# Recurrence gates as per-head products on quarters of the PE array, with the gated unit and the pool branch a step later and squares on ACT

## The chip, the cores and the metric

The kernel runs on one core of a Trainium2 chip. The metric is the device time of one execution in microseconds, the median of several runs. The time before is 2156.85 us, the median of 3 runs that lie between 2155.75 and 2157.89.

## What is computed

One block of a hybrid network on 2048 tokens of width 1024, in fp32: a modulated norm, a token mix of three branches, an output projection, then a convolutional feed-forward part. The change lies in the branches of the token mix: a two-way linear recurrence whose gates are 64 x 64 products per head, a pooling branch with one product per group, and a gated unit that mixes tokens inside chunks of 128.

```python
def block_diag(xh, w, b):
    y = jnp.einsum('blhi,hij->blhj', xh, w)
    return y.reshape(y.shape[0], y.shape[1], -1) + b

def rglru_coeffs(xf, w_a, b_a, w_x, b_x, lam):
    xh = xf.reshape(B, L, N_HEADS_A, HEAD_A)          # 8 heads of 64
    r = jax.nn.sigmoid(block_diag(xh, w_a, b_a))
    i = jax.nn.sigmoid(block_diag(xh, w_x, b_x))
    log_a = -LRU_C * r * jax.nn.softplus(-lam)
    a = jnp.exp(log_a)
    bterm = jnp.sqrt(-jnp.expm1(2.0 * log_a)) * (i * xf)
    return a, bterm                                    # h[t] = a[t] h[t-1] + bterm[t], both ways

def gmlp_group(z, norm_g, w_s, b_s):
    z = jax.nn.gelu(z)
    u, v = z[..., :D_C], z[..., D_C:]
    vn = (v - mean(v)) * rsqrt(var(v) + EPS) * norm_g
    s = jnp.einsum('gij,bnjgc->bnigc', w_s, vn_in_chunks_of_128) + b_s
    return u * s

def token_mix(z, y_rec, ...):
    ya = jax.nn.gelu(z[..., D_A:2 * D_A]) * y_rec
    yb = pool_group(...)        # mean over 2, 4, 8 or 16 tokens minus z, one product per group
    yc = gmlp_group(...)
    return jnp.concatenate([ya, yb, yc], axis=-1) @ w_out
```

## The kernel before, in words

Features lie on partitions, tokens on the free axis; tokens go in four chunks of CH = 512. Large products run as fp32 split into two f16 halves: `mm3` (L357 to L361) makes three f16 matmuls per 128 inputs, 24 for one output tile of a chunk. Small products (gates, pool, the token mix of the gated unit) run in fp32 directly.

The program is written with a scheduler that sets each engine's order from its own model of time; what comes ahead in the program has priority. `ORDER` (L38) is the list of steps that a loop walks through: `x` normalises a chunk, `c` is the recurrence of the 256 context tokens, `a` the projection and convolution of the recurrence's input, `f` and `b` a recurrence unit forward or backward for a chunk and a pair of head tiles (P is tiles 0 and 1, Q is 2 and 3), `G` the gelu gates with their squares, `g` a step of the gated unit, `p` a step of the pool branch, `m` steps of the later modulation, `i` and `w` weight preparation.

A recurrence unit (`lru_units`) calls `coeffs` for two head tiles: rp (L443) and ip (L444) are fp32 products of a 128 x 128 block-diagonal weight (two heads of 64 on the diagonal) with 512 tokens, ACT makes two sigmoids, then exponentials and roots with a table load between the kinds, POOL and DVE combine (L461, L463), and DVE scans (L479). There are 16 such units of two tiles, 8 forward and 8 backward, and the context has 8 sets of half width.

`gmlp` makes, for each of 8 steps, two tiles of 128 tokens: projection uv, gelu, normalisation on DVE, then the token mix sp (L623), bias and product on DVE, four transposes tp (L632) and a copy yc (L635) with its squares on ACT. `pool_br` (L539) projects a chunk (pl), adds shifted copies on DVE (L562 to L580) and multiplies the result, pb, with its weight (pp, L535); the product's result yb is read by DVE and squared there. `gates` (L639) multiplies the gelu of a projection gt with Y and squares the product. `vsumsq` (L153) squares and sums on DVE, `sumsq` (L150) on ACT. `wout_stats` squares the eight tiles of w_out, `prep_out` splits them in two f16 halves with `split` (DVE, L312 and L313); `split_ag` (L317 to L319) does the same with two ACT Copies and one POOL subtraction.

Of the kernel before, what the change touches and what calls it, by code (L numbers as in the profile page):

```python
# [18 lines left out]
CH = 512  # L19
# [21 lines left out]
m6 b3Q G3P p m6 w4 b2P G3Q p m6 w4 b2Q G2P p m6 w2 b1P G2Q p m6 w2 b1Q G1P p  # L41
# [27 lines left out]
def block_kernel(ctx: ExitStack, tc: tile.TileContext, x, xT, ctx_d, ctxT, cc, crow, cols_d, wm01, bm01, wmT,  # L69
# [104 lines left out]
    gwt = mix.tile([128, 4, 4, 128], F32, name="gwt")  # L174
# [47 lines left out]
    def stats_first(xt):  # L222
        acc = early.tile([128, CH], F32, tag="acc", name="acc")
# [216 lines left out]
    def coeffs(j, d, xa, w, c=None, bank=None):  # L440
        bank = pB if bank is None else bank
        rp, ip = bank("rp"), bank("ip")
        T.matmul(rp[:, :w], gwt[:, j, 2 * d, :], xa, start=True, stop=True)  # L443
        T.matmul(ip[:, :w], gwt[:, j, 2 * d + 1, :], xa, start=True, stop=True)  # L444
# [3 lines left out]
        act(i[:, :w], ip[:, :w], AF.Sigmoid, bias=col("bx", 4 * d + j))  # L448
# [90 lines left out]
    def pool_br():  # L539
        W = CH + 16  # L540
        for pt in range(2):
            prev = None
            yb = []
            for n in range(NCH + 1):
# [53 lines left out]
    def gmlp():  # L598
        ws = wslot["uv"]
        for tp in range(8):  # L600
            n, r = divmod(tp, 2)
            guvt = mix.tile([128, 2, CH], F32, tag="guv", bufs=2, name="guv")
            guv = [guvt[:, i, :] for i in range(2)]
            for i in range(2):
                t0 = tp * 256 + i * 128
                ps = pA("uv")
                mm3(ps, lambda k: hT[:, 0, k, t0:t0 + 128], lambda k: hT[:, 1, k, t0:t0 + 128],
                    lambda k: ws[k // 2][:, 0, k % 2, :], lambda k: ws[k // 2][:, 1, k % 2, :])
                act(guv[i], ps, AF.Gelu_apprx_tanh, scale=inv[:, 10:11])
                bst = small.tile([128, 6], F32, tag="bst", name="bst")  # L610
                V.bn_stats(bst, guv[i][:, 256:512])
                mv = small.tile([128, 2], F32, tag="mv", name="mv")
                V.bn_aggr(mv, bst)
                rs = small.tile([128, 1], F32, tag="rsv", name="rsv")
                rsqrt(rs, mv[:, 1:2], 1, 1.0)
                v = guv[i][:, 256:512]
                V.tensor_scalar(v, v, mv[:, 0:1], rs, op0=OP.subtract, op1=OP.mult)
                V.tensor_tensor(v, v, gnr, op=OP.mult)
                if i == 0:
                    yield  # L620
            sp = pC("sp")
            for g in range(4):
                T.matmul(sp[:, g * 128:(g + 1) * 128], wst[:, g, :], guvt[:, :, 256 + g * 64:320 + g * 64], start=True, stop=True)  # L623
            sv = sp.rearrange("p (g i c) -> p g i c", g=4, i=2)
            tp_ps = pC("tp")
# [608 lines left out]
```

## Time and profile before

| what | value |
|---|---|
| median of 3 runs | 2156.85 us (2155.75 to 2157.89) |
| profiled execution | 2155.6 us |
| span of the profile | 2153.8 us |
| PE busy | 2022.0 us, 94% of the span |
| DVE busy | 1593.2 us, 74% |
| ACT busy | 1194.6 us, 55% |
| POOL busy | 610.1 us, 28% |
| mean granted clock of PE | 0.972 of full speed |

Busy shares are means over stages with different limits. The page's 40 slices show PE at 6 to 9 tenths over the first quarter of the span and at 9 or more from there to the last slices; DVE stands at 9 tenths only in slices 7, 8 and 10. The first quarter holds the context, the forward and the backward recurrences; the output projection runs from about 553 to 770 us, the feed-forward part after it.

### The profile page before, as it was taken

To read this page: it belongs to the slowest core of one execution; us is meant where nothing else is said; L and a number is where in the kernel's file an instruction comes from. 1 tells how busy PE (TensorE), PEld (TensorE's weight loads), DVE (VectorE), ACT (ScalarE), POOL (GpSimd) and SP (SyncE) were. 2 spreads that over 40 slices of the span, in tenths; PEclk is the share of its full clock that TensorE was granted. 3 is DMA by queue.
4 is the path that set the end of the run, shared out by engine and by line. 5 is a ranking of instruction groups with operands and counts; after the bars stand their busy time and mean duration, and the time that the engine had idled before them with its cause. 6 is when DMAs were issued, how large, how long until landed. Compare 5 with 4: busy or idle time off the path is not lost.

```text
span 2153.8 us, 24277 instructions
## 1 busy us (share of the span) xinstructions
PE 2022.0 (94%) x9215; PEld 933.4 (43%) x9215; DVE 1593.2 (74%) x2214; ACT 1194.6 (55%) x1665; POOL 610.1 (28%) x457
## 2 busy tenths in 40 slices
PE   6878989788899998999999999999999999999995
PEld 1433444333455443444444444444444444444442
DVE  5687788999655359978667776867777686777876
ACT  4676756455254555656565554655556465555453
POOL 1233334445155510101121121212112121221156
PEclk8889999998999999999999999999999999999998
DMA  7521152512433210315455454544545454454248
GB/s 297 183 88 74 69 166 89 180 35 85 135 136 114 79 64 20 130 66 132 89 117 98 79 124 72 108 78 102 94 88 100 74 103 88 100 95 69 40 157 156
DMA packets 73480, 224.78 MB, mean 104 GB/s; under 512 B 7442, under 2 KB 18066, under 8 KB 68498
## 3 DMA queue, kind: packets, MB, share of 16 engines
q0 software_dynamic: 21312, 77.60, 21.4%
q1 hardware_dynamic: 52052, 145.64, 19.6%
q8 instruction: 72, 1.18, 0.2%
q14 instruction: 44, 0.36, 0.1%
HBM read 120.45 MB, written 102.76 MB: 104 GB/s over the span
## 4 chain that ended last, share of the span: by engine, by line
PE 55%; DVE 3%; POOL 1%; DMA 1%; ACT 1%; issue 1%; POOLq 0%; SPq 0%; DVEq 0%; ACTq 0%
PE up L359 12%; PE up L360 12%; PE up L361 12%; PE dn L1054 6%; PE dn L1056 6%; PE dn L1055 6%; DVE cv L1011 2%; DMA hT<-accd 1%; POOL hT L1069 0%; DVE hT L1086 0%; DVE hT L1060 0%; DMA wm<-in_wmT_dram 0%; POOL fms L159 0%; PE sct L121 0%; POOL out_dram L1087 0%
## 5 line engine op out<-in xcount | busy, mean ns | idle before, releaser
L1011 DVE SCALAR_TENSOR_TENSOR cv<-z,cols,cv 128x1008 f32<-128x1008 f32 (+3 forms) x704 | 870.4, 1250 | 276.6 <-ACT cv L1005 188.7
L359 PE MATMUL up<-hT,uw 128*128 128x512 f16 x1408 | 534.1, 379 | 2.6 <-ACT z L846 2.6
L361 PE MATMUL up<-hT,uw 128*128 128x512 f16 x1408 | 534.1, 379 | 0.0
L360 PE MATMUL up<-hT,uw 128*128 128x512 f16 x1408 | 534.1, 379 | 0.0
L1071 POOL DMA_DIRECT2D accd<-dd x132 | 114.2, 865 | 704.1 <-ACT dd L1065 697.9
L846 ACT ACTIVATE z<-up,upinv 128x512 f32<-128x512 f32 x176 | 120.5, 685 | 311.2 <-PE up L361 310.8
L1065 ACT ACTIVATE dd<-dn,gdi 128x512 f32<-128x512 f32 x320 | 214.2, 680 | 115.0 <-PE dn L1056 107.5
L1054 PE MATMUL dn<-dw,gs 128*128 128x512 f16 x704 | 267.2, 380 | 7.1 <-ACT dd L1065 5.3
L1055 PE MATMUL dn<-dw,gs 128*128 128x512 f16 x704 | 267.5, 380 | 0.0
L1056 PE MATMUL dn<-dw,gs 128*128 128x512 f16 x704 | 265.8, 380 | 0.0
L360 PEld LDWEIGHTS <-uw 128*128 128x128 f16 x1408 | 137.8, 98 | 167.5 <-issue 3.6
L359 PEld LDWEIGHTS <-uw 128*128 128x128 f16 x1408 | 139.0, 99 | 164.7 <-issue 0.6
L361 PEld LDWEIGHTS <-uw 128*128 128x128 f16 x1408 | 137.8, 98 | 166.5 <-issue 0.6
L832 POOL TENSOR_TENSOR uw<-ur,uw 128x2048 f16<-128x2048 f32 x22 | 89.5, 4070 | 168.9 <-ACT ur L831 168.9
L135 ACT ACT_TABLE_LOAD x77 | 98.8, 1283 | 47.4 <-PE rp L443 28.8
L1005 ACT ACTIVATE cv<-z,cols 128x1024 f32<-128x1024 f32 x88 | 106.0, 1206 | 2.0
L1055 PEld LDWEIGHTS <-gs 128*128 128x128 f16 x704 | 68.8, 98 | 86.8 <-issue 9.5
L1054 PEld LDWEIGHTS <-gs 128*128 128x128 f16 x704 | 72.2, 103 | 78.8 <-issue 0.8
L1056 PEld LDWEIGHTS <-gs 128*128 128x128 f16 x704 | 68.9, 98 | 83.5 <-issue 0.6
L986 POOL TENSOR_TENSOR dw<-dr,dw 128x1024 f16<-128x1024 f32 x22 | 46.4, 2127 | 141.8 <-PE dn L1056 100.3
L150 ACT ACTIVATE junk<-g 128x1024 bf16<-128x1024 f32 x44 | 46.3, 1053 | 59.9 <-DVE g L1019 59.9
L878 PE MATMUL wo<-wo,ysp 128*128 128x512 f16 x256 | 77.1, 383 | 1.0 <-ACT gm L807 1.0
(302 smaller groups left out, 3076.7 us busy)
## 6 DMA issues: line engine op xcount, KB each, us to landing
accd<-dd POOLq DMA_DIRECT2D x132, 512.0 KB, 5.1
ur<-in_wup_dram SPq DMA_DIRECT2D x22, 1024.0 KB, 5.6
wm<-in_wmT_dram SPq DMA_DIRECT2D x64, 256.0 KB, 2.9
dr<-in_wdn_dram SPq DMA_DIRECT2D x22, 512.0 KB, 4.6
hT<-in_wm_dram SPq DMA_DIRECT2D x8, 1024.0 KB, 14.4
xt<-in_xT_dram SPq DMA_DIRECT2D x8, 1024.0 KB, 7.1
ro<-in_wout_dram SPq DMA_DIRECT2D x16, 512.0 KB, 3.8
xr<-in_x_dram SPq DMA_DIRECT2D x16, 512.0 KB, 3.6
```

The source lines that it names most:

```text
L135: ins = A.activation(out_, in_, func, **kw).ins
L359: T.matmul(ps, wh(k), hh(k), start=(k == 0), stop=False)
L360: T.matmul(ps, wh(k), hl(k), start=False, stop=False)
L361: T.matmul(ps, wl(k), hh(k), start=False, stop=(k == KT - 1))
L846: A.activation(z[:, ab, b * 8:(b + 1) * 8, :], ps.rearrange("p (r x) -> p r x", x=64), AF.Identity, scale=upinv[:, c:c + 1])
L1005: A.activation(t, z[:, ab, r0:r0 + 16, :].rearrange("p r x -> p (r x)"), AF.Identity, bias=col("fcb", c + NP * ab), scale=wt(0, 0))
L1011: V.scalar_tensor_tensor(o, z[:, ab, ya + dy:yb + dy, xa + dx:xb + dx], wt(dy, dx), o, op0=OP.mult, op1=OP.add)
L1054: T.matmul(ps[h], hi, wh, start=i == 0, stop=False)
L1055: T.matmul(ps[h], hi, wl, start=False, stop=False)
L1056: T.matmul(ps[h], lo, wh, start=False, stop=i == n - 1)
L1065: A.activation(d[:, h * CH:(h + 1) * CH], ps[h], AF.Copy, scale=di)
L1071: G.dma_start(accd[t], d, accum_op=OP.add)
```

## The change

The gate weights keep only the 64 x 64 blocks, loaded by eight DMAs. For each set, rp and ip are four products, each on one quarter of the array; the two halves of ip lie swapped in its bank, and two sigmoids of 64 partitions swap them back. A step of the gated unit ends during the next one: sp follows the next tile's first projection, tp the second; its results go back into guv, which has three buffers in place of two. A pool step's product and squares are issued after the next step's projection. The squares of gates, pool and w_out move from DVE to ACT, and the split of w_out to ACT and POOL. gg has two buffers in place of three, acc uses the ring of xs, and the tile yc is dropped.

```diff
@@ ORDER
-m6 b3Q G3P p ... m6 w2 b1P G2Q p m6 w2 b1Q G1P p
+m6 b3Q G3P p ... m6 w2 b1P G2Q p m6 w2 b1Q G1P p g g
@@
-    gwt = mix.tile([128, 4, 4, 128], F32, name="gwt")
+    gwt = mix.tile([128, 4, 4, 64], F32, name="gwt")
+    HALVES = (slice(0, 64), slice(64, 128))
@@ stats_first
-        acc = early.tile([128, CH], F32, tag="acc", name="acc")
+        acc = early.tile([128, 2, CH], F32, tag="xs", bufs=2, name="acc")[:, 0, :]
@@ coeffs
-        T.matmul(rp[:, :w], gwt[:, j, 2 * d, :], xa, start=True, stop=True)
-        T.matmul(ip[:, :w], gwt[:, j, 2 * d + 1, :], xa, start=True, stop=True)
+        for h, o in zip(HALVES, HALVES[::-1]):
+            T.matmul(rp[h, :w], gwt[h, j, 2 * d, :], xa[h], start=True, stop=True)
+            T.matmul(ip[o, :w], gwt[h, j, 2 * d + 1, :], xa[h], start=True, stop=True)
...
-        act(i[:, :w], ip[:, :w], AF.Sigmoid, bias=col("bx", 4 * d + j))
+        for h, o in zip(HALVES, HALVES[::-1]):
+            act(i[h, :w], ip[o, :w], AF.Sigmoid, bias=col("bx", 4 * d + j)[h])
@@ pool_br
                     mm_in(ps, 8 + pt, n * CH, CH)
+                    if before is not None:
+                        before()
...
-                pool_out(b[:, lo:hi], hi - lo, pt, parts, "pp")
-                if n > 0:
-                    vsumsq(a[:, 0:CH], yb[n - 1], ysq[:, n - 1, 4 + pt:5 + pt])
+                def held(n=n, last=last, b=b, lo=lo, hi=hi, pt=pt, yb=yb):
...
+                    pool_out(b[:, lo:hi], hi - lo, pt, parts, "pp")
+                    if n > 0:
+                        sumsq(b[:, 0:CH], yb[n - 1], ysq[:, n - 1, 4 + pt:5 + pt])
+                if last:
+                    before()
+                    held()
+                before = held
@@ gmlp
-        for tp in range(8):
+        for tp in range(9):
...
             for i in range(2):
+                if tp < 8:
+                    gated(tiles[tp][:, i, :], tp * 256 + i * 128, ws)
+                if tp > 0 and i == 0:
...
+                if tp > 0 and i == 1:
...
+                    yc = guvt[:, :, 0:256]
+                    A.activation(yc, tp_ps.rearrange("p (c t) -> p c t", c=2), AF.Identity)
+                    sumsq(guvt[:, :, 256:512], yc, ysq[:, n, 6 + r:7 + r])
@@ gates
-                g = late.tile([128, CH], F32, tag="gg", bufs=3, name="gg")
+                g = late.tile([128, CH], F32, tag="gg", bufs=2, name="gg")
...
-                vsumsq(g, Y[n][:, j, :], ysq[:, n, j:j + 1])
+                sumsq(g, Y[n][:, j, :], ysq[:, n, j:j + 1])
@@ wout_stats, prep_out
-            vsumsq(r, r, t[:, k:k + 1])
+            sumsq(r, r, t[:, k:k + 1])
...
-        split(s[:, 0, :], s[:, 1, :], r, wosc)
+        split_ag(s[:, 0, :], s[:, 1, :], r, wosc)
@@ loads
-    S.dma_start(gwt, gw.rearrange("j p g c -> p j g c"))
+    for j in range(4):
+        for h in HALVES:
+            S.dma_start(gwt[h, j], gw[j, h, :, h])
```

Where the scheduler puts these instructions is seen in each engine's order. On PE, before, the gates of a backward unit stand between a projection of the pool (pl) and one of the gelu gates (gt), with the pool's product pp behind them; ws are f16 weights:

```order
L361 MATMUL pl_3015<-hT,ws_1883 128x512
L443 MATMUL rp<-Y_92,gwt 128x512
L444 MATMUL ip<-Y_92,gwt 128x512
L443 MATMUL rp<-Y_92,gwt 128x512 [waits Activation_49]
L444 MATMUL ip<-Y_92,gwt 128x512 [waits Activation_49]
L535 MATMUL pp<-pb,pwt 128x512 [waits DVE_49,PE_49]
L359 LDWEIGHTS ws_2022
L359 MATMUL gt_3121<-hT,ws_2022 128x512 [waits DVE_49]
```

In the change the four products of that place are eight of half the height and width, and pp is not among them:

```order
L362 MATMUL pl_2915<-hT,ws_1933 128x512
L446 MATMUL rp<-Y_92,gwt 64x512
L447 MATMUL ip<-Y_92,gwt 64x512
L446 MATMUL rp<-Y_92,gwt 64x512
L447 MATMUL ip<-Y_92,gwt 64x512
L446 MATMUL rp<-Y_92,gwt 64x512 [waits Activation_49]
L447 MATMUL ip<-Y_92,gwt 64x512 [waits Activation_49]
L446 MATMUL rp<-Y_92,gwt 64x512
L447 MATMUL ip<-Y_92,gwt 64x512
L360 LDWEIGHTS ws_2529
L360 MATMUL gt_3024<-hT,ws_2529 128x512 [waits Activation_49]
```

The pool's product that stood behind the gates is gone from this place; the gates are followed by gt at once.

The pool's third product pp stood, before, between matmuls of the gelu gate gt:

```order
L361 MATMUL gt_2984<-hT,ws_2489 128x512
L359 LDWEIGHTS ws_2489
L359 MATMUL gt_2984<-hT,ws_2489 128x512
L535 MATMUL pp<-pb,pwt 128x512 [waits DVE_49]
L360 LDWEIGHTS ws_2489
L360 MATMUL gt_2984<-hT,ws_2489 128x512
```

Now it stands inside the projection of the pool (pl) that, before, was done ahead of two gelu gates and came before that place; that projection is now its neighbour:

```order
L362 MATMUL pl_2915<-hT,ws_1933 128x512
L360 LDWEIGHTS ws_1933
L360 MATMUL pl_2915<-hT,ws_1933 128x512
L539 MATMUL pp<-pb,pwt 128x512 [waits DVE_49]
L361 LDWEIGHTS ws_1933
L361 MATMUL pl_2915<-hT,ws_1933 128x512
```

It has moved ahead, past the rest of that projection, a unit's gates and the better part of two gelu gates.

On ACT, before, a backward unit's exponentials and roots (lru) are followed by the gelus of two gate tiles (gg):

```order
L135 ACTIVATE lru<-lru,klam 128x512
L135 ACTIVATE lru<-lru,klam 128x512 [waits Activation_49]
L135 ACT_TABLE_LOAD
L135 ACTIVATE lru<-lru 128x512 [waits DVE_49] x2
L135 ACT_TABLE_LOAD
L135 ACTIVATE gg<-gt_3121,inv 128x512 [waits PE_49]
L135 ACTIVATE gg<-gt_3150,inv 128x512 [waits PE_49]
L135 ACT_TABLE_LOAD [waits PE_49,DVE_49,Activation_49]
```

Now each gelu is followed by the square of the product Y that DVE makes of it, and a square of the pool (into pb) stands ahead of the next table load:

```order
L135 ACTIVATE lru<-lru,klam 128x512
L135 ACTIVATE lru<-lru,klam 128x512 [waits Activation_49]
L135 ACT_TABLE_LOAD
L135 ACTIVATE lru<-lru 128x512 [waits DVE_49] x2
L135 ACT_TABLE_LOAD
L135 ACTIVATE gg<-gt_3193,inv 128x512 [waits PE_49]
L150 ACTIVATE gg,ysq<-Y_92 128x512 [waits DVE_49]
L135 ACTIVATE gg<-gt_3222,inv 128x512 [waits PE_49]
L150 ACTIVATE gg,ysq<-Y_92 128x512 [waits DVE_49]
L150 ACTIVATE pb,ysq<-yb 128x512 [waits DVE_49]
L135 ACT_TABLE_LOAD [waits PE_49]
```

Three squares have come in between the gelus and the next unit's sigmoids, each of them waiting for DVE.

On DVE, before, the pool's results yb are read, squared into pa, and the additions of the next pool step (L562 on) stand among squares of gates:

```order
L537 TENSOR_SCALAR yb<-pp,cols 128x8 [waits PE_49]
L537 TENSOR_SCALAR yb<-pp,cols 128x504
L153 SCALAR_TENSOR_TENSOR gg,ysq<-Y_92 128x512 [waits DVE_49]
L660 SCALAR_TENSOR_TENSOR wm,mcol<-wm,cb 128x512 [waits DMAHW4_49]
L514 COPY state<-lru 128x1 [waits DVE_49]
L153 SCALAR_TENSOR_TENSOR pa,ysq<-yb 128x512 [waits DVE_49]
L660 SCALAR_TENSOR_TENSOR wm,mcol<-wm,cb 128x512 [waits DMAHW5_49]
L562 TENSOR_TENSOR pa<-pz 128x527 [waits DVE_49]
L647 TENSOR_TENSOR Y_92<-gg,Y_92 128x512 [waits Activation_49]
L562 TENSOR_TENSOR pb<-pa 64x525 [waits DVE_49]
```

Now the squares are gone, and the first addition into pb waits for ACT:

```order
L518 COPY state<-lru 128x1 [waits DVE_49]
L541 TENSOR_SCALAR yb<-pp,cols 128x8 [waits PE_49]
L541 TENSOR_SCALAR yb<-pp,cols 128x504 [waits DMAHW7_49]
L568 TENSOR_TENSOR pb<-pa 64x525 [waits Activation_49]
L573 COPY pa<-pb 64x525 [waits DVE_49]
L683 SCALAR_TENSOR_TENSOR wm,mcol<-wm,cb 128x512 [waits DMAHW5_49]
L580 SCALAR_TENSOR_TENSOR pb<-pa,cols,pz 128x512 [waits DVE_49]
```

What DVE did between reading pp and the additions of the next step has moved to ACT, and a wait for ACT has come in.

## Rows read from the trace of the kernel before

**Rows 1.** Windows: us, busy PE, PEld, DVE, ACT, POOL (x), clock, DMA, GB/s.

```profile
140.00:358.00 218.00, 194.09 (x812) 90.87 (x812) 173.77 (x349) 147.65 (x203) 78.97 (x71) 0.94 0.25 86
358.00:553.00 195.00, 159.68 (x613) 70.73 (x613) 184.24 (x314) 93.64 (x119) 84.88 (x57) 0.91 0.34 107
...
1200.00:2000.00 800.00, 796.01 (x3728) 366.20 (x3727) 576.30 (x611) 452.12 (x563) 168.55 (x128) 1.00 0.48 92
```

**Rows 2.** Waits of PE, 140 to 553 us: us in total, times, longest.

```profile
PE pp L535 <- DVE pb L574: 23.1, 6, 6.6
PE tp L632 <- DVE guv L630: 19.2, 8, 6.4
```

**Rows 3.** Timeline of PE around a pool product: start us, us, [idle <-releaser].

```profile
406.97 0.38 PE L359 MATMUL gt<-hT,ws 128*128 128x512 f16 x1
412.41 2.08 PE L535 MATMUL pp<-pb,pwt 128*128 128x512 f32 x2 [5.07 <-DVE pb L574]
414.28 0.63 PE L360 MATMUL gt<-hT,ws 128*128 128x512 f16 x1
414.71 0.63 PE L361 MATMUL gt<-hT,ws 128*128 128x512 f16 x1
```

**Rows 4.** Groups by line and shape on DVE, 358 to 553 us.

```profile
L153 DVE SCALAR_TENSOR_TENSOR gg<-Y 128x512 f32<-128x512 f32 x16 | 15.0, 938 | 0.2
L153 DVE SCALAR_TENSOR_TENSOR ro<-ro 128x1024 f32<-128x1024 f32 x8 | 13.7, 1716 | 0.4 <-DMA ro<-in_wout_dram 0.4
L313 DVE SCALAR_TENSOR_TENSOR wo<-ro,wosc,wo 128x1024 f16<-128x1024 f32 x8 | 13.0, 1640 | 0.0
...
L153 DVE SCALAR_TENSOR_TENSOR pa<-yb 128x512 f32<-128x512 f32 x8 | 7.0, 880 | 0.0
...
L312 DVE TENSOR_SCALAR wo<-ro,wosc 128x1024 f16<-128x1024 f32 x8 | 5.9, 745 | 1.7 <-DMA ro<-in_wout_dram 1.6
...
L153 DVE DVE_READ_ACCUMULATOR gg<-Y 128x1 f32 x16 | 1.2, 77 | 0.0
```

**Rows 5.** Groups by line and shape on ACT, whole span: busy us, mean ns.

```profile
L985 ACT ACTIVATE dr<-dr,dnsc 128x1024 f32<-128x1024 f32 x22 | 24.1, 1134 | 0.0
...
L135 ACT ACTIVATE lru<-ip,cols 128x512 f32<-128x512 f32 x32 | 21.7, 677 | 0.1
...
L150 ACT ACTIVATE guv<-yc 128x512 f32<-128x512 f32 x8 | 5.0, 628 | 0.2
...
L150 ACT ACTIVATION_READ_ACCUMULATOR guv<-yc 128x1 f32 x8 | 1.5, 186 | 0.0
```

**Rows 6.** The same view on POOL.

```profile
L986 POOL TENSOR_TENSOR dw<-dr,dw 128x1024 f16<-128x1024 f32 x22 | 46.4, 2127 | 141.8 <-PE dn L1056 100.3 <-ACT dr L985 41.5
```

**Rows 7.** Timelines of PE and PEld at the gates of a backward unit.

```profile
395.19 1.02 PE L443 MATMUL rp<-Y,gwt 128*128 128x512 f32 x2
396.04 1.02 PE L444 MATMUL ip<-Y,gwt 128*128 128x512 f32 x2
...
398.62 0.38 PE L359 MATMUL gt<-hT,ws 128*128 128x512 f16 x1
...
395.62 0.19 PEld L444 LDWEIGHTS ip<-Y,gwt 128*128 128x128 f32 x1 [0.24 <-issue]
```

**Rows 8.** Groups by line and shape on PE, whole span.

```profile
L443 PE MATMUL rp<-Y,gwt 128*128 128x512 f32 x64 | 35.6, 640 | 6.5 <-DVE state L502 3.7 <-DVE Y L424 2.8
...
L269 PE MATMUL mps<-hT,ccol 128*2 128x512 f32 x64 | 30.0, 626 | 6.9 <-DMA hT<-in_wm_dram 6.9
```

**Rows 9.** Timeline of SP: issues of loads into xs.

```profile
28.92 1.91 SPq L246 DMA_DIRECT2D xs<-in_ctx_dram  x2
50.40 0.33 SPq L246 DMA_DIRECT2D xs<-in_x_dram  x1
```

**Rows 10.** Waits of ACT, 358 to 553 us: us in total, times, longest.

```profile
ACT lru L135 <- DVE lru L463: 30.6, 10, 7.0
ACT L135 <- PE rp L443: 27.8, 4, 9.3
```

More of the change, by code (lines that the diff above doesn't have):

```diff
@@ L40 @@
 g i89 f2Q g g i45 m6 f3P g g g g f3Q g g g m6 i67 m6 b3P p p p p
-m6 b3Q G3P p m6 w4 b2P G3Q p m6 w4 b2Q G2P p m6 w2 b1P G2Q p m6 w2 b1Q G1P p
+m6 b3Q G3P p m6 w4 b2P G3Q p m6 w4 b2Q G2P p m6 w2 b1P G2Q p m6 w2 b1Q G1P p g g
 m6 w2 b0P G1Q m6 w2 b0Q G0P m9 G0Q w9 w9
@@ L541, in pool_br @@
         for pt in range(2):
-            prev = None
+            prev, before = None, None
             yb = []
@@ L599, in gmlp @@
         ws = wslot["uv"]
-        for tp in range(8):
-            n, r = divmod(tp, 2)
-            guvt = mix.tile([128, 2, CH], F32, tag="guv", bufs=2, name="guv")
-            guv = [guvt[:, i, :] for i in range(2)]
-            for i in range(2):
[L605 to L625, printed above, removed]
-            bsb = col("bs", 0, 4)[:, :, None].to_broadcast([128, 4, 64])
-            for i in range(2):
-                v = guv[i][:, 256:512]
-                V.tensor_tensor(v.rearrange("p (g c) -> p g c", g=4), sv[:, :, i, :], bsb, op=OP.add)
-                V.tensor_tensor(v, v, guv[i][:, 0:256], op=OP.mult)
-                for ct in range(2):
-                    T.transpose(tp_ps[:, (ct * 2 + i) * 128:(ct * 2 + i + 1) * 128],
-                                v[:, ct * 128:(ct + 1) * 128], ident)
-            yc = mix.tile([128, 2, 256], F32, tag="yc", bufs=1, name="yc")
-            A.activation(yc, tp_ps.rearrange("p (c t) -> p c t", c=2), AF.Identity)
-            sumsq(guv[0].rearrange("p (c t) -> p c t", c=2), yc, ysq[:, n, 6 + r:7 + r])
-            S.dma_start(ybc[n][:, 2:4, r * 256:(r + 1) * 256], yc)
-            yield
@@ new lines, in gmlp @@
+        sv = None
+        tiles = {}
+        for tp in range(9):
+            n, r = divmod(tp - 1, 2)
+            if tp < 8:
+                tiles[tp] = mix.tile([128, 2, CH], F32, tag="guv", bufs=3, name="guv")
+            for i in range(2):
+                if tp < 8:
+                    gated(tiles[tp][:, i, :], tp * 256 + i * 128, ws)
+                if tp > 0 and i == 0:
+                    guvt = tiles[tp - 1]
+                    sp = pC("sp")
+                    for g in range(4):
+                        T.matmul(sp[:, g * 128:(g + 1) * 128], wst[:, g, :], guvt[:, :, 256 + g * 64:320 + g * 64],
+                                 start=True, stop=True)
+                    sv = sp.rearrange("p (g i c) -> p g i c", g=4, i=2)
+                    bsb = col("bs", 0, 4)[:, :, None].to_broadcast([128, 4, 64])
+                    for e in range(2):
+                        v = guvt[:, e, 256:512]
+                        V.tensor_tensor(v.rearrange("p (g c) -> p g c", g=4), sv[:, :, e, :], bsb, op=OP.add)
+                        V.tensor_tensor(v, v, guvt[:, e, 0:256], op=OP.mult)
+                if tp > 0 and i == 1:
+                    guvt = tiles.pop(tp - 1)
+                    tp_ps = pC("tp")
+                    for e in range(2):
+                        for ct in range(2):
+                            T.transpose(tp_ps[:, (ct * 2 + e) * 128:(ct * 2 + e + 1) * 128],
+                                        guvt[:, e, 256 + ct * 128:384 + ct * 128], ident)
+                    yc = guvt[:, :, 0:256]
+                    A.activation(yc, tp_ps.rearrange("p (c t) -> p c t", c=2), AF.Identity)
+                    sumsq(guvt[:, :, 256:512], yc, ysq[:, n, 6 + r:7 + r])
+                    S.dma_start(ybc[n][:, 2:4, r * 256:(r + 1) * 256], yc)
+                yield
@@ new lines, in gated @@
+    def gated(guv, t0, ws):
+        ps = pA("uv")
+        mm3(ps, lambda k: hT[:, 0, k, t0:t0 + 128], lambda k: hT[:, 1, k, t0:t0 + 128],
+            lambda k: ws[k // 2][:, 0, k % 2, :], lambda k: ws[k // 2][:, 1, k % 2, :])
+        act(guv, ps, AF.Gelu_apprx_tanh, scale=inv[:, 10:11])
+        v = guv[:, 256:512]
+        bst = small.tile([128, 6], F32, tag="bst", name="bst")
+        V.bn_stats(bst, v)
+        mv = small.tile([128, 2], F32, tag="mv", name="mv")
+        V.bn_aggr(mv, bst)
+        rs = small.tile([128, 1], F32, tag="rsv", name="rsv")
+        rsqrt(rs, mv[:, 1:2], 1, 1.0)
+        V.tensor_scalar(v, v, mv[:, 0:1], rs, op0=OP.subtract, op1=OP.mult)
+        V.tensor_tensor(v, v, gnr, op=OP.mult)
```

12 lines of the change are left out of this document (6 added, 6 removed).

## The prediction

> **What bounds the kernel now.** I read the windows first [rows 1], with the span cut where the work changes: context and first chunk to 140 us, forward recurrences to 358, backward recurrences to 553, then the output projection and the feed-forward part. From 1200 to 2000 us PE is busy for 796.01 of 800 us, one matmul per 0.2135 us (796.01 / 3728) at granted clock 1.00. So the last two thirds of the span are PE's, the change leaves their products alone, and what is won earlier arrives at the end as it is. In the backward stretch DVE is busy for 184.24 of 195 us (94%) and PE for 159.68; in the forward stretch PE has 194.09 of 218 and DVE 173.77. The change must be judged in these two stretches.
>
> The list of PE's waits [rows 2] says who holds PE there: the pool product pp waits for DVE's pb six times, 23.1 us in all, and the transposes tp wait for DVE's guv eight times, 19.2 us. The timeline shows one pp wait from near [rows 3]: 5.07 us of idle PE, then gt matmuls that start 0.43 us apart (414.28 to 414.71) and last 0.63, where they last 0.38 before: a lower granted clock for some microseconds (the backward stretch's mean is 0.91) that makes a wait dearer than it looks.
>
> **The change, part by part.** *Squares and wout off DVE.* From the rows of DVE in the backward stretch [rows 4] go the gate squares (16, 15.0 us), the pool squares (8, 7.0), the squares of wout (8, 13.7) and the two halves of wout's split (13.0 and 5.9): 54.6 us, with their accumulator reads, 77 ns for each of 32, 57.0. The gated unit's last step moves in: four operations of 256 columns, each under the 0.938 us of a 512-wide one, 2.4 by my estimate. DVE falls from 184 to about 130 us and is no longer the bound.
>
> They land on ACT and POOL, priced by like rows [rows 5, 6]. A 512-wide square is 0.628 us and its accumulator read 0.186, so 24 squares of gates and pool cost 19.5. A 1024-wide square has the Copy row's width (1.134), so 8 of them with reads cost 10.6; 16 Copies of wout cost 18.1. The second sigmoid of ip adds at most 0.677 for each of 14 coefficient sets, 9.5; and two late gmlp steps a Copy, a square and a read each, 2 x (2 x 0.628 + 0.186) = 2.9. Together 60.6: ACT goes from 93.64 to about 154 us, the highest load of the stretch. POOL gets 8 subtractions of 2.127 us, 17.0, and stands at 102. PE needs about 145 us there at full clock (159.68 x 0.91). The stretch can therefore end anywhere between 154 us (ACT without a gap) and the present 195 or somewhat above. I take **172**: that is 195 less the 23.1 us of pp waits, and it is also ACT's 154 with 12% of idle time, which I hold for the least of an engine that runs in order behind PE and DVE and loads a table between its kinds of work; DVE, the present bound, has 6%. Gain 23, ends 0 and 41.
>
> *Pool branch a step later.* In PE's new order the third pp has moved ahead by the rest of a projection, a unit's gates and most of two gelu gates, so the order counts on a DVE that is ready earlier; a lighter DVE is, and if it isn't, the wait stays. The squares of the pool now write into pb, which has one buffer, so DVE's next addition waits for ACT; that wait is new for six steps, lies on a 0.8 us square, and has the pp wait's 23.1 us as the price at which nothing would be won. It is in the 12%.
>
> *Gated unit a step later.* The 19.2 us of tp waits are the most that this can give, and below nothing is excluded only by the order: nothing queues behind tp but the matmuls that stood before it. Of the eight tp, the new order has three with only gate products and up to 11 matmuls between their sp and them (about 3 to 6 us), the others with 24 to 28 matmuls (5 to 6 us) or more, where the old distances of 25 to 35 matmuls still left waits of up to 6.4 us. I take 5 us, ends 0 and 19.
>
> *Quarter products, PE.* One fp32 product is two MATMUL records [rows 7]: rp starts at 395.19, the next at 396.04, and four end with the first gt at 398.62, (398.62 - 395.19) / 4 = 0.857 us each, or 0.43 a pass, with the weight load of the next (0.19 us) under the running pass. For a head tile and direction that is 1.71 us now, for 32 of them 54.9, and 8 of half width in the context, with half the tokens half of that each, 6.9. The new form has four products of two passes. A quarter's own two passes must follow one another, for they stream the same rows into the same columns, and products are issued in order. So the second pass of one product can run beside the first of the next, and no more: one pass per product, 4 x 0.43 = 1.71 us, **as now**. What a smaller array piece costs no row shows; the nearest is mps, which uses 2 of 128 columns and lasts 626 ns per record, as rp with its 640 does [rows 8]: narrowness alone buys nothing. Ends: 0.857 and 3.43 us (the two rivals below).
>
> The page "TensorEngine Tiling (Array Packing)" of the Trainium skill (Key Properties) says that tiles load weights and multiply independently of one another, which speaks for the lower end; on the trace of before it can't be seen, since nothing there uses part of the rows. The same section says that a change of tiling mode drains the array.
>
> *Small costs.* A matmul lasts 0.38 us and its successor starts after 0.2135, so an emptied pipeline costs some 0.17 us; entering and leaving the quarters for 20 units is 40 x 0.17 = 6.8 us at most, zero at least. The context's eight extra sigmoids and gwt's eight DMAs ahead of the context's loads add little: those DMAs stand on SP ahead of xs, issued at 28.92 us, but ACT gives xs free again only for the issue at 50.40 [rows 9]; about 20 us of cover, and without it their issue time of a few microseconds would show. I take 3 us for all of this, ends 0 and 12. The 18 sigmoid halves of the forward stretch (12.2 us at most) fall beside PE: ACT has 147.65 of 218 us there. The output projection's order is the same, the first feed-forward groups are shuffled a little: nothing.
>
> **Sum.** Against the profiled execution's 2155.6 us: -23 - 5 + 0 + 3 gives 2130.6. The median of the runs stands 1.25 above that execution, so **2132**; own range 2114 to 2146.
>
> **Rivals.** *R1, the quarters run together.* If all four products stream beside each other, two passes (0.857 us) do the work of four. The 18 sets of the forward stretch, where PE is nearest to full, save 0.86 us each, 15 us, of which I count 11, the context 3; the backward stretch is ACT's and saves little. Time about 2118. For it: the four use four different quarters. Against it: the two passes of each product in order. The page "TensorE: Matmul & The Clock Gate" of the Trainium skill (Measured speedup vs the span model) gives 3.07x for four row tiles of 512 columns; by it R1 would hold, and no run here shows such tiles.
>
> *R2, the quarters run one after another (slower).* If a quarter's matmul waits for the one before it, each product costs the full 0.857 us, since mps shows no discount: 3.43 us per set, 1.71 more. The forward stretch grows by 18 x 1.71 = 31, less 7 that the gated unit's gain and old waits take; the context by 5; PE in the backward stretch needs 145 + 24 = 169 us, which with the waits that are left is about 188 in place of 172. Time 2155.6 + 24 + 5 - 7 = 2178, by the median 2179 (2160 to 2190). For it: weights are loaded twice as often, and rp and ip of one half, which follow each other, share their moving rows. Against it: at full width the load runs under the matmul [rows 7]. It decides from about 2.6 us per set on: 29 sets' worth (forward, context, half of backward) x 0.87 is the 25 us that the rest gives. The same page of the Trainium skill (The mechanism) has weights load under a running matmul only where the row groups differ, which speaks against this order; the trace of before shows the contrary for the whole array, 0.19 us of load within a 1.02 us pair.
>
> *R3, ACT takes DVE's place.* Each gate square stands in ACT's queue and waits for DVE's product, with the next unit's sigmoids behind it; ACT waits in the backward stretch already for DVE's L463 (30.6 us) and PE's rp (27.8) [rows 10]. If 40 us of waits stay beside its 154 us of work, the stretch is 194 and only 2 to 5 us are won in all: about 2153, range 2146 to 2164. For it: it's now the fullest engine, and its table sets forbid much reordering. Against it: what it waits for, DVE, gets 54 us lighter. More than 18 us of idle time makes the forecast too low.
>
> **How the numbers follow.** A measurement of this kernel tells about 0.2% (4.3 us) from no change: faster is below 2152.5, slower above 2161.2. Chances: forecast 0.47, R1 0.16, R3 0.16, R2 0.21. Faster: 0.46 + 0.16 + 0.06 of R3 = 0.68; same: 0.01 + 0.08 of R3 + 0.02 of R2 = 0.11; slower: 0.02 of R3 + 0.19 of R2 = 0.21. The range of 2108 to 2170 leaves out some 0.13 of R2 and thin tails.
>
> **What would show it.** Right: rp and ip records of the quarters that start about 0.43 us apart per product, ACT above 145 us and DVE below 140 in the backward stretch, a stretch of 165 to 180 us, pp waits below 8 us in all. Wrong: quarter sets that take under 1.2 us (R1) or over 2.6 (R2), or a backward stretch above 185 with ACT's waits on DVE above 40 us (R3). A feed-forward part that is not 1600 us long as now would upset the sum altogether.

## The result, and the profile after

The changed kernel takes 2168.28 us (median of 5 runs, 2165.95 to 2170.88) beside 2156.85 for the kernel before in the same series: a ratio of 1.0053, 95% interval 1.0039 to 1.0068. It is slower by 11 us, where 2132 was forecast. The time lies within the range that was given (2108 to 2170), near its upper end; the sign is wrong.

The page of the changed kernel shows that the work did move as the change says, busy time and instructions of each engine:

```profile
span 2167.1 us, 24668 instructions
## 1 busy us (share of the span) xinstructions
PE 2006.8 (93%) x9375; PEld 913.9 (42%) x9375; DVE 1534.6 (71%) x2134; ACT 1266.5 (58%) x1785; POOL 621.7 (29%) x465
```

To see where the time went, both traces are cut at the same events: the first gate product of the first backward unit, and the first product of the output projection. Windows of the changed kernel (columns as in [rows 1]):

```profile
0.00:351.80 351.80, 272.44 (x1265) 117.20 (x1266) 245.48 (x549) 232.07 (x347) 110.63 (x104) 0.88 0.38 135
351.80:569.50 217.70, 171.39 (x762) 72.54 (x762) 146.55 (x253) 160.91 (x232) 100.80 (x72) 0.88 0.31 99
569.50:2167.10 1597.60, 1562.92 (x7352) 724.13 (x7352) 1142.55 (x1335) 873.56 (x1207) 410.29 (x289) 0.99 0.43 97
```

and of the kernel before, cut at the same events:

```profile
0.00:335.70 335.70, 279.35 (x1159) 128.38 (x1160) 249.16 (x534) 213.06 (x320) 107.00 (x102) 0.91 0.39 142
335.70:553.05 217.35, 179.29 (x706) 80.67 (x705) 203.42 (x350) 109.30 (x142) 95.62 (x67) 0.92 0.32 102
553.05:2153.80 1600.75, 1563.32 (x7352) 724.30 (x7352) 1140.63 (x1333) 872.27 (x1205) 407.46 (x288) 0.99 0.43 97
```

The span is 13.3 us longer: the part up to the backward units lost 16.1, the backward part 0.35, the rest gained 3.15. In the backward part DVE has 56.9 us less to do and ACT 51.6 more, and it takes as long as before. In the part ahead of it PE is busy for 7 us less and yet the part is 16 us longer. So, taken together, the work taken off PE and off DVE brought nothing. The two can't be judged from this pair of traces, since the second sigmoid lies in the same stretches; the experiments part them.

The gates themselves went better than forecast. PE's timeline at a backward unit (columns as in [rows 3]) shows the four products of a set side by side:

```profile
441.52 0.38 PE L362 MATMUL pl<-hT,ws 128*128 128x512 f16 x1
441.82 0.64 PE L446 MATMUL rp<-Y,gwt 64*64 64x512 f32 x1
441.83 0.64 PE L447 MATMUL ip<-Y,gwt 64*64 64x512 f32 x1
441.84 0.64 PE L446 MATMUL rp<-Y,gwt 64*64 64x512 f32 x1
441.85 0.64 PE L447 MATMUL ip<-Y,gwt 64*64 64x512 f32 x1
442.31 0.59 PE L446 MATMUL rp<-Y,gwt 64*64 64x512 f32 x1
...
442.73 0.59 PE L446 MATMUL rp<-Y,gwt 64*64 64x512 f32 x1
```

The first passes of the four products start 10 ns apart, the second passes of all four 0.49 us later, and the next set after another 0.42: 0.91 us for a set that took 1.71 [rows 7]. PE has the gates ready earlier; the delay is on ACT. ACT's timeline of the same unit, in the changed kernel:

```profile
444.30 0.69 ACT L135 ACTIVATE lru<-rp,cols 128x512 f32<-128x512 f32 x1
445.03 0.72 ACT L135 ACTIVATE lru<-lru,klam 128x512 f32<-128x512 f32 x1
445.77 1.38 ACT L135 ACTIVATE lru<-ip,cols 64x512 f32<-64x512 f32 x2
447.17 0.69 ACT L135 ACTIVATE lru<-rp,cols 128x512 f32<-128x512 f32 x1
447.88 1.38 ACT L135 ACTIVATE lru<-ip,cols 64x512 f32<-64x512 f32 x2
449.29 0.72 ACT L135 ACTIVATE lru<-lru,klam 128x512 f32<-128x512 f32 x1
450.03 1.28 ACT L135 ACT_TABLE_LOAD   x1
451.32 1.33 ACT L135 ACTIVATE lru<-lru,klam 128x512 f32<-128x512 f32 x2
```

and a unit of the kernel before:

```profile
426.41 0.69 ACT L135 ACTIVATE lru<-rp,cols 128x512 f32<-128x512 f32 x1
427.13 0.72 ACT L135 ACTIVATE lru<-lru,klam 128x512 f32<-128x512 f32 x1
427.76 0.67 ACT L135 ACTIVATE lru<-ip,cols 128x512 f32<-128x512 f32 x1
428.33 0.68 ACT L135 ACTIVATE lru<-rp,cols 128x512 f32<-128x512 f32 x1
428.90 0.69 ACT L135 ACTIVATE lru<-ip,cols 128x512 f32<-128x512 f32 x1
429.47 0.73 ACT L135 ACTIVATE lru<-lru,klam 128x512 f32<-128x512 f32 x1
430.21 1.28 ACT L135 ACT_TABLE_LOAD   x1
431.51 1.33 ACT L135 ACTIVATE lru<-lru,klam 128x512 f32<-128x512 f32 x2
```

From the first sigmoid to the end of the exponentials the unit needs 452.65 - 444.30 = 8.35 us, before 432.84 - 426.41 = 6.43. A sigmoid of 64 partitions takes as long as one of 128, so each of the two sets pays 0.7 us more; wider spacing of the instructions adds another half microsecond. ACT's group by line says it for all 32 sets (as [rows 5]):

```profile
L135 ACT ACTIVATE lru<-ip,cols 64x512 f32<-64x512 f32 x64 | 43.7, 683 | 1.1
```

That is 22.0 us more than the 32 whole sigmoids of 677 ns [rows 5], all of it between a unit's products and its scans. The context's eight sets of half width add 3.7 us more (7.5 in place of 3.8).

The waits changed hands. PE's from 140 us to the end of the backward part at 569.5 us (as [rows 2]):

```profile
PE sct L121 <- DVE gsfmm L298: 13.0, 1, 13.0
PE rp L446 <- DVE Y L425: 9.8, 3, 6.2
PE pp L539 <- DVE pb L580: 9.6, 4, 5.8
PE rp L446 <- DVE Y L422: 8.4, 2, 4.4
PE tp L640 <- DVE guv L634: 7.5, 3, 5.6
PE ip L447 <- ACT gg L135: 7.1, 1, 7.1
PE sp L627 <- DVE guv L661: 6.8, 3, 3.6
PE pp L539 <- DVE pb L586: 6.4, 3, 3.5
PE uv L360 <- ACT guv L135: 6.1, 1, 6.1
PE pp L539 <- issue: 5.6, 1, 5.6
```

and two that the kernel before had beside those of [rows 2]:

```profile
PE sct L121 <- DVE gsfmm L297: 4.6, 1, 4.6
PE pp L535 <- DVE pb L580: 4.0, 1, 4.0
```

and ACT's in the changed kernel's backward part (as [rows 10]):

```profile
ACT gg L150 <- DVE Y L670: 25.6, 13, 4.7
ACT ro L150 <- DMA ro<-in_wout_dram: 13.6, 5, 5.9
ACT lru L135 <- DVE lru L467: 9.3, 9, 2.8
```

pp waits 9.6 us for the sum that it waited 23.1 for [rows 2] (L574 before is L580 now), but with its other waits it still stands for 21.6 us, beside 27.6 before (23.1, 4.0 and one of 0.5). tp waits 7.5 in place of 19.2. New or longer are the gate products' waits for the convolved input Y in the forward stretch (18.2 us, before 2.8), sp's for DVE, those for ACT, and the last wait of the backward part, sct's for DVE's statistics (13.0 for 4.6). ACT waits 9.3 us for DVE's combination L467 where it waited 30.6 [rows 10], but 25.6 for the product Y ahead of a gate's square, and 13.6 for w_out's loads.

### The profile page after: what moved, and what is told of

Same layout as the page of the kernel before. It is cut to its first block, busy times and chain, and to the rows that moved or that the text cites. A ratio compares the mean times of both kernels' runs of the same rounds, so it can differ in the third digit from the quotient of the medians.

```text
span 2167.1 us, 24668 instructions
## 1 busy us (share of the span) xinstructions
PE 2006.8 (93%) x9375; PEld 913.9 (42%) x9375; DVE 1534.6 (71%) x2134; ACT 1266.5 (58%) x1785; POOL 621.7 (29%) x465
## 4 chain that ended last, share of the span: by engine, by line
PE 54%; DVE 3%; POOL 1%; DMA 1%; issue 1%; ACT 1%; POOLq 0%; SPq 0%; DVEq 0%; ACTq 0%
PE up L360 12%; PE up L361 12%; PE up L362 12%; PE dn L1079 6%; PE dn L1081 6%; PE dn L1080 6%; DVE cv L1036 2%; DMA wm<-in_wmT_dram 1%; POOL hT L1094 0%; DVE hT L1111 0%; DMA hT<-accd 0%; DVE hT L1085 0%; POOL dw L1011 0%; POOL fms L159 0%; DVE g L1044 0%
## 5 line engine op out<-in xcount | busy, mean ns | idle before, releaser
L1036 DVE SCALAR_TENSOR_TENSOR cv<-z,cols,cv 128x1008 f32<-128x1008 f32 (+2 forms) x704 | 870.8, 1250 | 272.4 <-ACT cv L1030 182.8
```

The lines of the kernel that those rows point to most:

```text
L1036: V.scalar_tensor_tensor(o, z[:, ab, ya + dy:yb + dy, xa + dx:xb + dx], wt(dy, dx), o, op0=OP.mult, op1=OP.add)
```

## The experiments

Seventeen kernels were run, each beside the kernel before on the same chip. "Quarters" are the four products on four quarters with ip swapped, "diagonal" the two diagonal quarters only. e6 and e12 leave out the swap back of ip's halves, and e13 leaves out the exponential; they compute something else and are there for the time alone.

| run | kernel | median us | ratio to before (95%) |
|---|---|---|---|
| e1 | before + quarters | 2165.82 | 1.0048 (1.0031, 1.0065) |
| e2 | after, full products | 2156.78 | 1.0007 (0.9995, 1.0020) |
| e3 | before + squares and w_out off DVE | 2154.57 | 1.0002 (0.9991, 1.0013) |
| e4 | after, squares and w_out on DVE | 2169.38 | 1.0065 (1.0049, 1.0082) |
| e5 | before + split sigmoid | 2163.04 | 1.0043 (1.0031, 1.0056) |
| e6 | before + quarters, one sigmoid | 2151.97 | 0.9986 (0.9977, 0.9994) |
| e7 | before + eight loads | 2151.17 | 0.9985 (0.9977, 0.9994) |
| e8 | before + diagonal | 2152.18 | 0.9991 (0.9982, 1.0000) |
| e9 | e8 + third lru buffer | 2158.70 | 1.0016 (1.0007, 1.0025) |
| e10 | e8 + w_out off DVE | 2156.12 | 1.0004 (0.9994, 1.0014) |
| e11 | e9 + w_out off DVE | 2152.46 | 0.9991 (0.9978, 1.0005) |
| e12 | after, one sigmoid | 2147.99 | 0.9969 (0.9959, 0.9979) |
| e13 | before, exp replaced by sigmoid | 2141.80 | 0.9937 (0.9923, 0.9950) |
| e14 | before + split gelus | 2157.65 | 1.0013 (1.0005, 1.0022) |
| e15 | after, diagonal | 2152.31 | 0.9986 (0.9975, 0.9998) |
| e16 | e8 + tanh gates | 2138.24 | 0.9915 (0.9901, 0.9929) |
| e17 | e15 + tanh gates | 2136.51 | 0.9917 (0.9904, 0.9931) |

The kernel before had medians of 2154.07 to 2154.66 in these series and 2156.85 in that of the result, so kernels of different series are compared by what they stand above or below it. Every kernel is ordered anew by the scheduler, so some us of any difference can come from an order that fell out otherwise: 2.9 in e7, whose edit adds no work, and perhaps 6 in e9 beside e8.

**Which part loses.** Four kernels first: the quarters alone on the kernel before, the change without them, the move off DVE alone, and the change without that move.

```diff
+ e1: before.py with coeffs(), gwt and its loads as in the change
+ e2: the changed kernel with coeffs(), gwt and its load as before
+ e3: before.py with sumsq for vsumsq in gates, pool_br and wout_stats, split_ag for split in prep_out
+ e4: the changed kernel with vsumsq and split in those places
```

> The kernel before with the quarter products alone (gate weights, eight products per unit, two sigmoid halves for ip). Theory A (the squares on ACT are what costs the change its gain; the quarters run side by side and save PE 0.86 us per set of gates): the forward stretch, where PE is busiest, keeps part of 0.86 x 18 = 15 us, 2143 to 2152 us. Theory B (the quarters cost as much as they save: 40 more sigmoid halves on ACT, shorter cover, lower clock): 2155 to 2165 us.

> The changed kernel with the gates as full 128 x 128 products again, all else as changed. Theory A: the saving of the quarters is lost, 2173 to 2182 us. Theory B: 2158 to 2168 us, at or below the changed kernel's 2168.

> The kernel before with only the squares of gates, pool and w_out on ACT and w_out's split on ACT and POOL; no step is delayed, gates are full products. Theory A (ACT's in-order queue waits for DVE's product ahead of each square and holds up the next unit): no gain or a loss though DVE gets 57 us lighter, 2156 to 2170 us. Theory B: DVE's relief shows, 2130 to 2148 us.

> The changed kernel with all squares of gates, pool and w_out and the split of w_out back on DVE; quarters and the two delays stay. Theory A: ACT is free again and the quarters' saving shows, 2145 to 2158 us. Theory B: DVE is full again in the backward stretch, 2166 to 2185 us.

The quarters alone give the whole loss (1.0048 beside the change's 1.0053), and without them the change is as fast as the kernel before (1.0007). Moving the squares and w_out is worth nothing in the kernel before (e3) and at most 3.6 us in the changed one (e4 beside the change). Theory A, mine after the first look, fell; theory B's direction held: the quarters cost. e2's 2156.78 lies just below B's range, and e3's 2154.57 between the two, so B's gain from a lighter DVE did not show either.

**What of the quarters costs.** They bring a second sigmoid per set, products on parts of the array, and eight loads; each was tried by itself.

```diff
+ e5: for h in (slice(0, 64), slice(64, 128)):
+         act(i[h, :w], ip[h, :w], AF.Sigmoid, bias=col("bx", 4 * d + j)[h])
+ e6: e1 with act(i[:, :w], ip[:, :w], AF.Sigmoid, bias=col("bx", 4 * d + j))
+ e7: for j in range(4):
+         for h in (slice(0, 64), slice(64, 128)):
+             S.dma_start(gwt[h, j], gw[j, h])
+ e8: for h in HALVES: T.matmul(rp[h, :w], gwt[h, j, 2 * d, :], xa[h], start=True, stop=True)
+     for h in HALVES: T.matmul(ip[h, :w], gwt[h, j, 2 * d + 1, :], xa[h], start=True, stop=True)
```

> The kernel before with full gate products, but ip's sigmoid made in two unswapped halves of 64 partitions, each as long as the whole. Theory C (the extra sigmoid per set, 0.69 us, lengthens the chain of recurrence units, which follow one another through two lru buffers and ACT: 2 x 0.69 x 16 = 22 us at most): 2162 to 2172 us. Theory D (it is the quarters on PE that cost: lower clock, waits moved to worse places): 2153 to 2159 us.

> The kernel before with the quarter products and ip's halves swapped in their bank, but one sigmoid of 128 partitions over them, so that i belongs to the other head (the swap back is left out). Theory C: the loss goes and some of PE's 0.86 us per set shows, 2140 to 2154 us. Theory D: the loss stays, 2160 to 2168 us.

> The kernel before with the full gate weights loaded by eight DMAs in place of one, nothing else. Theories C and D: the same as before, 2152 to 2159 us. Theory E (the eight issues on SP delay the context's loads and with them all that follows): 2160 to 2168 us.

> The kernel before with 64 x 64 products on the two diagonal quarters only: rp of both heads side by side, then ip of both heads, no swap, one sigmoid each. PE should need 1.71 us per set as with full products. Theory C: 2152 to 2159 us, as before. Theory D (work on part of the array is what costs): 2160 to 2168 us.

The split sigmoid with full products costs 9.0 us (2163.04 beside 2154.07); the quarters without it cost nothing. So it's the sigmoid (theory C), not PE or the loads. A lower granted clock, theory B's other reason, isn't it either: e5 has the loss at a mean clock of 0.970 to 0.974, as before, and e12 below has none of it at 0.964 to 0.969. The diagonal form is the test of PE's part. Its timeline, columns as in [rows 3]:

```profile
391.93 1.07 PE L446 MATMUL rp<-Y,gwt 64*64 64x512 f32 x4
392.84 1.02 PE L448 MATMUL ip<-Y,gwt 64*64 64x512 f32 x4
393.69 1.02 PE L446 MATMUL rp<-Y,gwt 64*64 64x512 f32 x4
```

Two products run side by side, and a set takes 393.69 - 391.93 = 1.76 us, as a full one did. With twice the PE time of e6 the kernel takes the same time (2152.18 and 2151.97): PE's saving in the gates is worth nothing on the kernel before.

**What the units wait for.** A chain through the two lru buffers was my reason for the sigmoid's price; a third buffer and the relief of DVE were to show it.

```diff
+ e9: mix.tile(shape, dt, tag="lru", bufs=3, name=name), with acc, gg and yc as in the change
+ e10: sumsq in wout_stats and split_ag in prep_out
+ e11: both
```

> The kernel of the diagonal quarters with a third buffer for the recurrence's coefficients (lru), paid for with the smaller gate weights, acc in the ring of xs, two gg buffers and yc written into guv. Theory C (the recurrence units follow one another through two lru buffers, and this chain sets the pace of the forward and backward stretches): the next unit's first tile starts before the last one's scans are done, 2120 to 2145 us. Rival F (PE's order and DVE set the pace, the buffers are not what the units wait for): 2149 to 2157 us, as the diagonal quarters' 2152.

> The kernel of the diagonal quarters with only w_out's squares on ACT and its split on ACT and POOL, 32 us off DVE in the backward stretch, and none of this work waits for DVE. Theory G (relief of DVE is worth time where the moved work does not wait for DVE's products, as the gate squares do): 2138 to 2149 us. Theory C: work on or off DVE is off the chain, 2149 to 2156 us.

> Both together: three lru buffers, and w_out's squares and split off DVE. Theory C: with the chain loosened DVE is the bound of the backward stretch and its relief counts, 2110 to 2138 us, below each of the two alone. Rival F: 2145 to 2156 us.

Beside the kernel before, e8 stands at -1.9 us, e9 at +4.3, e10 at +1.7 and e11 at -2.0: no gain on e8 from either or from both, and with the third buffer alone a loss of 6 us, beyond both ranges, whose cause is open (it also has one gg buffer less). Nothing shows that the buffers are what a unit waits for. This part of theory C fell; its other part, that time on a unit's way through ACT counts, had to be tested without the buffers.

**Time on the units' way through ACT, and beside it.**

```diff
+ e12: the changed kernel with act(i[:, :w], ip[:, :w], AF.Sigmoid, bias=col("bx", 4 * d + j))
+ e13: act(c[0][:, :w], c[0][:, :w], AF.Sigmoid, scale=c[4])      # in place of AF.Exp
+ e14: for h in (slice(0, 64), slice(64, 128)):                   # gmlp, and so in gates
+          act(guv[i][h], ps[h], AF.Gelu_apprx_tanh, scale=inv[h, 10:11])
```

> The changed kernel with one sigmoid of 128 partitions over ip, whose halves lie swapped (the swap back is left out, so i belongs to the other head); all else as changed. Theory C (the second sigmoid per set is the loss): 2153 to 2160 us, the 2156.8 of the changed kernel with full gates or a little less. Theory I (in the changed kernel the loss has other sources beside the sigmoids): 2162 to 2168 us.

> The kernel before with the exponential of each recurrence unit replaced by a sigmoid (so a is wrong), which needs no table load of its own: 1.28 us of ACT less on each unit's path, 16 units and 4 of the context. Theory C, with the 0.41 us per us of ACT time that the split sigmoids cost: 25 x 0.41 = 10 us less, 2141 to 2149 us. Theory J (only what is queued on PE and DVE counts, and the split's cost came from the order that the scheduler then chose): 2151 to 2158 us.

> The kernel before with the 32 gelus of the gates and of the gated unit made in two halves of 64 partitions each: as many more ACT instructions as the split sigmoids of the recurrence (32 of some 0.69 us, 22 us), but not in the recurrence units. Theory C (what counts is time on the units' path): 2153 to 2158 us. Theory H (any 22 us more on ACT cost as much): 2161 to 2166 us.

The changed kernel with one sigmoid stands 6.7 us below the kernel before (2147.99 to 2154.66), the change 11.4 above it: 18.1 us between them, more than I had expected. Taking 1.28 us of table load off each unit's way gives 12.9 us (2154.66 to 2141.80), in the traces all of it ahead of the backward units. Some 22 us of extra ACT work in the gelus cost 3.0, where the split sigmoids, 22 us and 3.7 in the context, cost 9.0. This fits theory C, that time between a unit's products and its scans is what is passed on, but it doesn't show it: the 6 us between e5 and e14 are no more than e9 differs from e8, and in the backward stretch of the traces both lose the same (last part of this section). That the second sigmoid makes the loss is shown, by e5 in the kernel before and by e12 in the changed one; by which waits it does so is argued.

**Kernels that keep the lesson.**

```diff
+ e15: the changed kernel with e8's products, one sigmoid per gate
+ e16, on e8, and e17, on e15:
+     act(r[:, :w], rp[:, :w], AF.Tanh, scale=0.5, bias=hb[:, 4 * d + j:4 * d + j + 1])
+     act(i[:, :w], ip[:, :w], AF.Tanh, scale=0.5, bias=hb[:, 8 + 4 * d + j:9 + 4 * d + j])
+     act(t[:, :w], r[:, :w], AF.Tanh, scale=k, bias=k)           # k is half of what it was
+     act(c[0][:, :w], c[0][:, :w], AF.Exp, scale=c[4], bias=c[4])
+     V.scalar_tensor_tensor(i[:, :w], i[:, :w], 1.0, xa, op0=OP.add, op1=OP.mult)
+     act(c[2][:, :w], c[2][:, :w], AF.Sqrt, scale=-0.25)
```

> The changed kernel with the products on the two diagonal quarters: rp of both heads, then ip of both heads, no swap, one sigmoid each; all else as changed, and nothing is left out. Theory C (the second sigmoid is the loss, PE's time in the gates counts little): 2146 to 2156 us, near the 2148 with one sigmoid. Theory K (the 2148 came from PE's 0.86 us per set, which this form gives back): 2154 to 2162 us.

> The kernel before with diagonal quarters and the sigmoids of the recurrence written as tanh, so that sigmoid, tanh and exp need one table set: one table load of 1.28 us less per unit, as with the exponential replaced, but the reference is computed. The product of i and xa moves from POOL to DVE (32 of some 0.9 us). Theory C: the 12.9 us of the replaced exponential less what DVE's added work takes, 2140 to 2150 us. Theory J (time on the units' ACT path is not what counts): 2152 to 2162 us.

> The same tanh form on the changed kernel with diagonal quarters, where DVE has some 57 us less to do in the backward stretch. Theory C: the two gains add, 2133 to 2145 us, the fastest of all. Theory J: as the changed kernel with diagonal quarters or slower, 2148 to 2160 us.

e15 is the change without its loss, 2.0 us below the kernel before. PE's saving in the gates, 32 x 0.85 = 27 us, is worth the 4.7 us between it and e12 (6.7 below) there, or 9.1 beside e2's full products (2.4 above). e16 computes the sigmoids as (1 + tanh) / 2, so that a unit's gates and its exponentials need one table. ACT's groups count 59 table loads in e16 where the kernel before had 77:

```profile
L135 ACT ACT_TABLE_LOAD x59 | 75.7, 1283 | 1.8 <-PEq L1232 0.7
...
L135 ACT ACT_TABLE_LOAD x77 | 98.8, 1283 | 47.4 <-PE rp L443 28.8 <-DVE state L514 12.7 <-DMA hfd<-lru 3.8
```

It takes 2138.24 us, 16.1 less than the kernel before (ratio 0.9915), and e17 2136.51. These are the fastest of the study and beat both kernels. By the medians the gains of e15 and e16 add (2.0 and 16.1, e17 17.8); by the ratios (0.9915 and 0.9917) e16 and e17 can't be told apart. That exp and tanh share a table, the page "ScalarE: Activation LUTs" of the Trainium skill states (Table sets: the hidden batching unit); the 18 loads that went agree.

**Where each kernel wins and loses.** Cut at the same two events as above, the traces, one execution each, give (us):

| run | up to the backward units | backward part | DVE busy in it | ACT busy in it | rest |
|---|---|---|---|---|---|
| before | 335.7 | 217.4 | 203 | 109 | 1600.8 |
| e3 | 337.7 | 215.9 | 159 | 150 | 1597.4 |
| e2 | 343.9 | 211.1 | 147 | 146 | 1597.8 |
| e5 | 338.2 | 225.7 | 202 | 123 | 1598.1 |
| e14 | 334.4 | 225.2 | 199 | 122 | 1598.6 |
| e13 | 322.4 | 220.4 | 202 | 98 | 1597.5 |
| e12 | 339.5 | 211.2 | 146 | 147 | 1598.9 |
| after | 351.8 | 217.7 | 147 | 161 | 1597.6 |
| e8 | 334.0 | 216.8 | 201 | 109 | 1598.0 |
| e15 | 344.4 | 208.5 | 151 | 146 | 1598.7 |
| e16 | 323.4 | 209.6 | 198 | 101 | 1596.8 |
| e17 | 336.3 | 200.5 | 152 | 139 | 1598.4 |

The lines of e3 and e5 for the backward part, and of e12 for the two parts (columns as in [rows 1]):

```profile
337.70:553.60 215.90, 178.16 (x706) 80.21 (x704) 159.15 (x279) 150.18 (x222) 105.67 (x75) 0.92 0.33 104
...
338.20:563.90 225.70, 180.11 (x707) 81.16 (x706) 202.41 (x353) 122.92 (x160) 97.50 (x68) 0.90 0.32 99
...
0.00:339.50 339.50, 272.65 (x1262) 116.07 (x1262) 252.50 (x549) 213.79 (x323) 110.99 (x104) 0.88 0.40 140
339.50:550.70 211.20, 170.03 (x763) 71.84 (x763) 146.06 (x251) 146.50 (x216) 104.71 (x72) 0.89 0.32 102
```

A trace can stand some us from its kernel's median: e12's execution took 3.4 us more and e14's 2.3, e16's 6.6 less. Three things can be read from them even so. First, 44 us less work on DVE alone (e3) shorten the backward part by 1.5 us. Second, the change without its quarters (e2), and so e15 beside e8 and e17 beside e16, wins 6 to 9 us in the backward part and loses 8 to 13 ahead of it. e3, which has the squares and w_out alone, loses 2 there, so what loses is most likely the gated unit's delay or the shared buffers that come with it; no run parts these. Third, the second sigmoid costs 2.5 us ahead of the backward units and 8.3 in the backward part in the kernel before (e5), but 12.3 and 6.5 in the changed one (after beside e12).

## Why the prediction was wrong, step by step

Two steps failed: the 23 us that the backward stretch was to give back, and the price of the second sigmoid, which was put at nothing ahead of the backward stretch and taken as covered within it. With the gated unit's 5 us, which did not come either, they account for about the 36 us between 2132 and 2168.

**Bounds.** That the feed-forward part passes on what is won or lost earlier held: 1600.75 us before, 1597.60 after. That DVE bound the backward stretch did not. It was busy for 94% of it [rows 1]; without 44 us of its work (e3) the stretch was 1.5 us shorter, and with the two delays as well (e2) 6 us. A busy share near one was taken for a bound. (The page has DVE at 9 tenths in slices 8 to 10, counted from one, which lie in this stretch, and in 16 and 17, not in 7, 8 and 10.)

**The sums of work** were near: DVE was to fall by 54.6 us net and fell by 56.9; ACT was to gain 60.6 and gained 51.6 over the shifted part. **The gain of 23 us from them was the first step that failed.** I took the pp waits for time that would be given back. Of pp's 27.6 us 6.0 went, and other waits came: ACT now waits 25.6 us for Y ahead of the squares. R3 named this wait, and e3, which has this part alone, came out at 2154.57, near R3's 2153: relief and new waits are about even.

**The second sigmoid** is the step that turned the sign. I priced it as 9.5 us within ACT's load in the backward stretch, covered by the 12% of idle time, and at nothing in the forward stretch, "beside PE: ACT has 147.65 of 218 us there". By e5 it costs 9.0 us in the kernel before, by e12 18.1 in the changed one, where 12.3 us of it lie ahead of the backward units. ACT's idle time was no cover. The reason that I would give, not shown by a run of its own, is that the halves stand in a row with the unit's exponential, its combination and its root, and ACT is idle because it waits within that row. Why the price is higher in the changed kernel stays open. A fuller ACT in the backward part (161 of 218 us busy, before 109) doesn't explain it: the extra cost lies ahead of that part, where ACT is as busy in e5 (228 of 338 us) as in the change (232 of 352).

**Quarter products, PE.** "One pass per product, as now" failed: all four products ran at once, 0.91 us per set, as in R1. R1's time of 2118 failed too, since PE's 27 us are worth nothing on the kernel before (e6 beside e8) and some 5 to 9 us in the changed one (e12 beside e15 and e2). R2, the way I gave to a slower kernel, was not it: the array did what the change wants. The range held the measured time because it had been stretched for R2 and R3; that the time lies in it is luck.

**Gated unit, 5 us.** tp waits went from 19.2 to 7.5 us, more than forecast, but sp brought 6.8, uv 6.1 (before 2.5) and the gate products' waits for Y 18.2 (before 2.8); e2, with this and the pool's delay and the squares, is 2 us from the kernel before. Nothing was won in all: what e2 wins in the backward part it loses ahead of it.

**Small costs, 3 us.** The eight loads cost nothing; e7 is 2.9 us faster with them.

## What to carry to other kernels

An instruction added to a serial row (gate, exponential, root, scan) isn't free because its engine has idle time: follow one unit through all engines and count what stands between its first input and what releases the next, and run the instruction alone, as e5 does. An engine that is 94% busy may still be no bound; the test is to take a fifth of its work away, as e3 does, with nothing else changed. Cut the traces at the same events: a change that looks like nothing in the total (e2) had won in one stretch and lost in another. Splitting a product to save PE time must not be paid for by one more instruction behind it, for on ACT half the partitions cost the whole duration.

## What the runs showed of the hardware that I had not expected

- Four fp32 products on four quarters ran at once though each is two passes: starts within 30 ns, 0.91 us for a set that took 1.71 on the whole array. The two diagonal quarters took 0.85 to 0.91 per pair. The page "TensorEngine Tiling (Array Packing)" of the Trainium skill (Key Properties) says that tiles run independently; the trace agrees.
- Going in and out of the quarters cost about 0.1 us each: the first quarter product started 0.30 us after the last full matmul (441.52 to 441.82), where full ones follow at 0.2135 and a full fp32 product at 0.22 (394.97 to 395.19). The first quarter's weight load began only with its product, at 441.82; that of the full product lay under the matmul ahead of it, from 394.97 on. On the way out gt started 0.52 us after the last quarter pass (443.18 to 443.70), where quarter passes follow at 0.42.
- A tanh needed no table load behind a gelu: in e16 the first gate of a unit starts at 407.07 us with only a gelu ahead of it (400.46), and the load comes behind that set's third activation, at 409.20.
- Eight loads of the gate weights in place of one made the kernel before 0.15% faster (ratio 0.9985, 0.9977 to 0.9994). Its cause is open; the scheduler's order on PE hardly differs.
